# Gate and up projections as seven half-size products of 2x2 blocks, with two of the four weight sums made by accumulating transfers

## The chip, the core and the metric

The kernel runs on one core of one Trainium2 chip. A core has TensorE (matmuls, results in PSUM), VectorE (DVE in the profile), ScalarE (ACT), GpSimd (POOL) and SyncE (SP, which here only issues transfers), one instruction stream each, synchronised by semaphores, and 16 DMA engines. The metric is the device time of one launch in microseconds, as the median of several runs.

## The reference

One encoder layer on 512 tokens of 1024 channels, all in float32: a mixing part (a gated linear recurrence branch and a delta-rule branch), then a SwiGLU feed-forward part, with RMS norms. What the change touches is the feed-forward part:

```
x = x + (g_rnn * y_rnn + g_dn * y_dn) @ w_out[l]
h = rmsnorm(x, ffn_norm[l])
gu = h @ w_gate_up[l]                    # 1024 x 5632
gt, up = jnp.split(gu, 2, axis=-1)       # 2816 columns each
x = x + (jax.nn.silu(gt) * up) @ w_down[l]
return rmsnorm(x, final_norm)
```

## The kernel before

All large products are made from float32 operands split in a high part (rounded to the matmul's fp32r format) and a low part (what is left), as three matmuls: high by high, high by low, low by high. Activations lie with channels on partitions and the 512 tokens along the free dimension.

`Plan` (L56) records every instruction of all engines first, with an estimated cost, a wanted time (`plan.t`) and the tiles that it touches. `order` (L147) then makes a list schedule: each engine takes the most urgent instruction whose operands and tile buffers are there, and the instructions are emitted in that order, fixed for each engine. `spend` (L431) moves the wanted time on by the time that TensorE is to take, and starts a new stage; the first 172 stages, all up to the output projection, have their priorities in the list `TIMES`, the later ones go by the running time. Weights are loaded some 40 us ahead of their wanted time and split `AHEAD` = 12 us ahead. A transfer is planned with its issue cost, 1.4 us, its bytes at 360 GB/s times 1.25, and 0.9 us; VectorE's and ScalarE's costs are taken 10% high, POOL's 20%. `Rec.call` (to L372) holds the costs and makes every instruction, so nearly all rows of the profile have the line L372, and groups are told apart by tiles.

The tiles: `wraw` (3 buffers, a weight block as loaded), `whi` and `wlo` (2 each, its parts), `graw` (1), `t2` (14 of 128x512) and `t4` (22 of 128x1024); both of the last appear as `t` in the profile. PSUM has 3 banks `mm`, 3 `ax` and 2 `st`.

The feed-forward part: `norm_transpose` (L488) scales and transposes two chunks of 128 tokens at a time on TensorE (by a diagonal matrix `dg`), and makes `hh2` and `hl2`, high and low parts (ScalarE the high, VectorE the low). Then, for each of `NF` = 22 blocks of 128 outputs, gate and up (L1195 on): load a 1024x128 block (512 KB) on SP's queue, cast it on ScalarE, subtract on VectorE, and accumulate 24 matmuls of 512 columns in `mm3` (L589), or twice 24 of 256 columns for the first two blocks (`parts` 2), so that the first can begin before all tokens are normed. After both, ScalarE makes the silu, VectorE the product, and `split` its two parts, in `fa[n]`. The down projection (L1211 on) goes over pairs of these blocks, in two halves of 512 output columns, with each chunk of tokens as the stationary operand.

Of the kernel before, what the change touches and what calls it, by code (L numbers as in the profile page):

```python
# [10 lines left out]
ALU = mybir.AluOpType  # L11
# [44 lines left out]
class Plan:  # L56
    """Records the engines' instructions in program order, then emits them in the order of a list schedule: each engine
    takes the most urgent instruction whose operands and tile slots are there."""
# [8 lines left out]
    def __init__(self, nc):  # L67
        self.nc = nc
        self.ops = []
        self.where, self.bases = [], []  # L70
        self.t = self.base = 0.0
        self.stage = 0
        self.tags = {}
        self.tile_tag = {}
        self.hist = {}
        self.keep = set()
        self.extra = ()
        self.admit = ()

# [242 lines left out]
class Rec:  # L322
    """One engine of a Plan: a call is recorded, not made."""
# [4 lines left out]
    def __getattr__(self, op):  # L328
        real = getattr(self.real, op)

        def call(*a, **kw):
# [46 lines left out]
def trunk(ctx: ExitStack, tc: tile.TileContext, x, mix_norm, w_in, rg_conv_w, rg_conv_b, rg_wa, rg_ba, rg_wx, rg_bx,  # L378
# [64 lines left out]
    # ------------------------------------------------------------ constants  # L443
# [16 lines left out]
    # ------------------------------------------------------------ x, norm, transpose  # L460
# [27 lines left out]
    def norm_transpose(srcs, dgs, gain_, hh, hl, c0):  # L488
        """Two chunks of tokens, scaled, to channels on partitions, times the norm's weights, in high and low parts."""
        for k2 in range(KD // 2):  # L490
# [28 lines left out]
    # ------------------------------------------------------------ per-channel parameters  # L519
# [45 lines left out]
    # ------------------------------------------------------------ projections  # L565
# [3 lines left out]
    def stage(src, shape, view=lambda t: t, admit=()):  # L569
        """A block of weights in its high and low parts: the load and the split run ahead of the products."""  # L570
# [46 lines left out]
    # ------------------------------------------------------------ DeltaNet gates, token-major, columns (dir, head, chunk)  # L617
# [61 lines left out]
    # ------------------------------------------------------------ RG-LRU  # L679
# [67 lines left out]
    # ------------------------------------------------------------ gates and branch projections  # L747
# [9 lines left out]
    # ------------------------------------------------------------ DeltaNet  # L757
# [112 lines left out]
        # back to rows on partitions: tb[0] the inverses, tb[1] their transposes  # L870
# [16 lines left out]
        # level 64  # L887
# [28 lines left out]
        # level 128  # L916
# [123 lines left out]
    # ------------------------------------------------------------ order of the mixing part  # L1040
# [99 lines left out]
    # ------------------------------------------------------------ output projection, residual, norm  # L1140
# [41 lines left out]
    ws = [weights_w(wo_part(k2, 1)) for k2 in range(4)]  # L1182
    for c in range(NT):
# [5 lines left out]
        if c % 2:  # L1189
            norm_transpose(x1[c - 1:c + 1], dgs[c - 1:c + 1], gain2, hh2, hl2, c - 1)  # L1190
# [3 lines left out]
    fa = []  # L1194
    for n in range(NF):  # L1195
        pos = []
        for c0 in (n * P, D_FF + n * P):
            spend(5.2)
# [6 lines left out]
        V.tensor_tensor(s_, s_, pos[1], ALU.mult)  # L1205
# [4 lines left out]
    ssf = small([P, NT, 3], "ssf", 1)  # L1210
    def down_mm(po, c, k2, hi, lo, n0=0, n=512):  # L1211
        spend(1.3 * n / 512)
        cs_ = slice(c * P, (c + 1) * P)
        for k in (2 * k2, 2 * k2 + 1):
            T.matmul(po[:, 0:n], fa[k][:, 0, cs_], hi[:, k % 2, n0:n0 + n], start=k == 0, stop=False)
            T.matmul(po[:, 0:n], fa[k][:, 0, cs_], lo[:, k % 2, n0:n0 + n], start=False, stop=False)
            T.matmul(po[:, 0:n], fa[k][:, 1, cs_], hi[:, k % 2, n0:n0 + n], start=False, stop=k == NF - 1)
# [10 lines left out]
    # (chunk, first column, columns) of each accumulation: the last one's end is all that the output waits for  # L1228
# [65 lines left out]
```

## Time and profile before

| | |
|---|---|
| median of 3 runs | 1113.97 us (1112.96 to 1114.12) |
| span of the profiled execution | 1112.2 us |
| mean granted TensorE clock | 0.998 |
| second norm and blocks 0 and 1 of gate and up | 740.6 to 767.5 us |
| blocks 2 to 21 | 767.5 to 985.1 us |
| down projection, last norm, stores | 985.1 to 1112.2 us |

The rows of the profile give start, duration, engine, operation, the written tile, the read tiles, shape and count. Groups give the busy time and the mean in ns, then the idle time of that engine just before them and what ended it. A matmul's duration is its time through the array; matmuls overlap, so the time that one costs is the distance between starts. PEld is TensorE's weight load.

### The profile page before, as it was taken

How to read it: one execution, taken by the hardware profiler on the slowest of the kernel's cores; microseconds unless marked ns; L12 is line 12 of the kernel's file. 1: busy time of each engine (PE TensorE's matmuls, PEld its weight loads, DVE VectorE, ACT ScalarE, POOL GpSimd, SP SyncE). 2: the span in 40 equal slices, each digit the busy share in tenths (PEclk: the TensorE clock that was granted, in tenths of full speed). 3: DMA queues.
4: the chain of work that ended last, by engine and by line, in shares of the span. 5: the costliest groups of instructions: out<-in, count | busy, mean ns of one | idle time of the engine just before them, and what ended most of it. 6: DMA issues, size and time to landing. Idle time of an engine off the chain costs nothing.

```text
span 1112.2 us, 15808 instructions
## 1 busy us (share of the span) xinstructions
PE 1087.8 (98%) x6228; PEld 915.5 (82%) x6228; DVE 703.1 (63%) x1230; ACT 577.1 (52%) x1000; POOL 44.5 (4%) x93
## 2 busy tenths in 40 slices
PE   7999999999999999999999999999999999999997
PEld 6988788878888887888788796889888888888886
DVE  5777999699985988698579748653333333332432
ACT  6868988876358546584754434343323232321223
POOL 2000000002010100210010000000000000000000
PEclk9999999999999999999999999999999999999999
DMA  7342323223321142023212213513333333323322
GB/s 196 91 112 76 95 77 93 73 78 107 85 77 53 29 138 77 22 74 95 59 34 78 82 36 129 175 38 95 95 95 95 95 98 102 104 89 101 114 95 76
DMA packets 160778, 98.29 MB, mean 88 GB/s; under 512 B 4800, under 2 KB 151344, under 8 KB 160704
## 3 DMA queue, kind: packets, MB, share of 16 engines
q1 hardware_dynamic: 159232, 93.99, 29.6%
q10 hardware_dynamic: 1184, 3.15, 0.8%
q8 instruction: 49, 0.80, 0.3%
q0 software_dynamic: 288, 0.13, 0.1%
q14 instruction: 25, 0.20, 0.1%
HBM read 95.17 MB, written 2.10 MB: 87 GB/s over the span
## 4 chain that ended last, share of the span: by engine, by line
PE 83%; DVE 3%; ACT 2%; issue 0%; DVEq 0%; ACTq 0%
PE mm L372 59%; PE st L372 12%; PE ax L372 12%; DVE t L372 3%; ACT na L372 1%; ACT t L372 1%; DVE wlo L372 0%; ACT ax L372 0%; ACT whi L372 0%; ACT L372 0%; DVE na L372 0%; DVEq L1289 0%; ACT drt L372 0%; ACT rst L372 0%; DVE nq L372 0%
## 5 line engine op out<-in xcount | busy, mean ns | idle before, releaser
L372 DVE TENSOR_TENSOR wlo<-wraw,whi 128x1024 fp32r<-128x1024 f32 (+2 forms) x171 | 196.1, 1148 | 264.8 <-PE mm L372 147.8
L372 PE MATMUL mm<-hh,whi 128*128 128x512 f32 (+2 forms) x896 | 334.1, 378 | 1.1 <-ACT whi L372 1.1
L372 PE MATMUL mm<-hl,whi 128*128 128x512 f32 (+2 forms) x896 | 333.8, 377 | 0.0
L372 ACT CAST whi<-wraw 128x1024 fp32r<-128x1024 f32 (+2 forms) x172 | 169.8, 988 | 286.3 <-PE mm L372 202.3
L372 PE MATMUL mm<-hh,wlo 128*128 128x512 f32 (+1 forms) x880 | 211.5, 378 | 1.1 <-DVE wlo L372 1.1
L372 PEld LDWEIGHTS mm<-hh,whi 128*128 128x128 f32 (+1 forms) x896 | 167.9, 187 | 31.2 <-ACT whi L372 1.9
L372 PEld LDWEIGHTS mm<-hl,whi 128*128 128x128 f32 (+1 forms) x896 | 167.9, 187 | 29.5 <-DVE hl L372 0.2
L372 DVE TENSOR_TENSOR t<-t,t 128x512 fp32r<-128x512 f32 (+18 forms) x365 | 173.5, 485 | 26.8 <-ACT t L372 22.4
L372 PEld LDWEIGHTS mm<-hh,wlo 128*128 128x128 f32 x880 | 158.0, 188 | 31.1 <-DVE wlo L372 1.5
L372 PE MATMUL mm<-t,whi 128*128 128x512 f32 x320 | 81.8, 397 | 2.6 <-ACT t L372 1.8
L372 DVE SCALAR_TENSOR_TENSOR t<-mm,par,t 128x511 f32<-128x511 f32 (+1 forms) x108 | 79.7, 741 | 3.6 <-ACT t L372 2.9
L372 ACT ACT_TABLE_LOAD x58 | 74.4, 1283 | 5.8 <-PEq L1280 1.7
L372 PEld LDWEIGHTS mm<-t,whi 128*128 128x128 f32 x320 | 59.9, 190 | 17.0 <-ACT t L372 2.4
L372 ACT CAST t<-t 128x512 fp32r<-128x512 f32 x62 | 38.3, 617 | 64.5 <-DVE t L372 64.2
L372 PE MATMUL ax<-t,t 32*32 32x32 f32 (+3 forms) x642 | 57.9, 254 | 0.6 <-issue 0.5
L372 PEld LDWEIGHTS ax<-t,t 32*32 32x32 f32 (+1 forms) x642 | 44.7, 139 | 8.0 <-ACT t L372 1.6
L372 PE MATMUL st<-whi,t 128*128 128x512 f32 (+1 forms) x152 | 46.8, 367 | 0.0
L372 PE MATMUL ax<-whi,t 128*128 128x512 f32 (+1 forms) x152 | 46.6, 366 | 0.0
L372 ACT ACTIVATE t<-t 128x128 f32<-128x128 f32 (+3 forms) x64 | 37.4, 602 | 15.2 <-DVE t L372 12.1
L372 PE MATMUL mm<-t,wlo 128*128 128x512 f32 x160 | 43.1, 396 | 0.0
L372 PE MATMUL st<-hh,whi 128*128 128x512 f32 (+1 forms) x112 | 42.1, 380 | 0.0
L372 PE MATMUL st<-hl,whi 128*128 128x512 f32 (+1 forms) x112 | 41.8, 377 | 0.0
(172 smaller groups left out, 1299.0 us busy)
## 6 DMA issues: line engine op xcount, KB each, us to landing
wraw<-in_w_in_dram SPq DMA_DIRECT2D x72, 512.0 KB, 3.9
wraw<-in_w_gate_up_dram SPq DMA_DIRECT2D x44, 512.0 KB, 3.9
wraw<-in_w_down_dram SPq DMA_DIRECT2D x22, 512.0 KB, 3.7
wraw<-in_w_rnn_proj_dram SPq DMA_DIRECT2D x16, 384.0 KB, 3.4
wraw<-in_w_out_dram SPq DMA_DIRECT2D x8, 512.0 KB, 4.6
wraw<-in_w_dn_proj_dram SPq DMA_DIRECT2D x8, 384.0 KB, 3.4
t<-in_x_dram SPq DMA_DIRECT2D x4, 512.0 KB, 5.1
na<-in_x_dram ACTq DMA_DIRECT2D x4, 512.0 KB, 7.2
```

Source lines behind the costliest of these rows:

```text
L372: self.plan.add(e, lambda: real(*a, **kw), outs, ins, cost, tail, table)
```

## The change

For blocks 2 to 21, gate and up together are seen as one 2x2 block product. The weight is [[G1, G2], [U1, U2]], where G is the gate's and U the up projection's block of 128 outputs, and 1 and 2 are the halves of the 1024 inputs; the activation has the two halves of the inputs by the two halves of the tokens, 256 each. Seven products of a 512x128 weight by a 512x256 activation take the place of eight. They need four sums of weights, here named t1 = G1 + U1, t3 = U1 + U2, t2 = t1 + U2 and t4 = t2 + G2, four differences of activations, made once, and additions of the results.

- t1 and t3 come from transfers: SP loads G1 and U1 into the two halves of one `wraw` tile, and POOL's queue adds U1 and U2 onto them in the tile (`accum_op`). t2 and t4 are VectorE adds. G is loaded whole and split as before; U2 is loaded by itself in `graw`. Seven weights are split in parts, on ScalarE and VectorE.
- `norm_transpose` also writes an unsplit copy of the second norm's result (`whole`) in four `t4` tiles, from which the differences `q5`, `q7`, `q6`, `q3` are made and split while blocks 0 and 1 run. Those two blocks both go in halves of 256 columns, as before.
- The output of a block is left unsplit in `fa`, with the two token halves swapped for odd blocks, and is split a pair at a time in the down projection (`split_pair`); part of the low halves takes the place of `hh2` and `hl2`.
- The planner's fixed cost of one fp32r matmul is 13.3 ns, for 2.5, from the second half of the output projection on.

Comments are taken out too, which does nothing. The core of the diff:

```diff
-                    cost = max(n / 2.4, 107 if rhs.dtype == F32R else 54) + 2.5
+                    cost = max(n / 2.4, 107 if rhs.dtype == F32R else 54) + (self.plan.fixed if rhs.dtype == F32R else 2.5)
...
                 V.scalar_tensor_tensor(hl[:, kt, c0 * P:(c0 + 2) * P], pv, gain_[:, kt:kt + 1], f(ho), ALU.mult, ALU.subtract)
+                if whole:
+                    A.activation(whole[kt // 4][:, kt % 4, :], pv, AF.Copy, scale=gain_[:, kt:kt + 1])
...
     ws = [weights_w(wo_part(k2, 1)) for k2 in range(4)]
+    plan.fixed = 13.3
+    a1 = [four(shape=(P, 4, 256)) for _ in range(2)]
+    a2 = [four(shape=(P, 4, 256)) for _ in range(2)]
...
+    def parts_of(src, hi, lo, ahead):
+        now = plan.t
+        plan.t = now - ahead
+        A.copy(hi, src)
+        V.tensor_tensor(lo, src, f(hi), ALU.subtract)
+        plan.t = now
...
-            mm3(po, hi, lo, lambda k: hh2[:, k, :], lambda k: hl2[:, k, :], KD, 2 if n < 2 else 1)
+            mm3(po, hi, lo, lambda k: hh2[:, k, :], lambda k: hl2[:, k, :], KD, 2)
...
-        y = four(F32R)
-        split(s_, y)
-        fa.append(y)
...
+    (a11, a12), (a21, a22) = a1, a2
+    q5, q6, q7, q3 = (four(shape=(P, 4, 256)) for _ in range(4))
+    qs = {}
+    for name, q, x_, y_ in (("5", q5, a21, a22), ("7", q7, a11, a21), ("6", q6, a11, q5), ("3", q3, a12, q6)):
+        V.tensor_tensor(q, x_, y_, ALU.subtract)
+        qh, ql = four(F32R, (P, 4, 256)), four(F32R, (P, 4, 256))
+        A.copy(qh, q)
+        V.tensor_tensor(ql, q, f(qh), ALU.subtract)
+        qs[name] = (qh, ql)
...
+    def product(po, w, x_, start):
+        (wh, wl), (xh, xl) = w, x_
+        for k in range(4):
+            T.matmul(po, wh[:, k, :], xh[:, k, :], start=start and k == 0, stop=False, skip_group_check=not start)
+            T.matmul(po, wh[:, k, :], xl[:, k, :], start=False, stop=False, skip_group_check=not start)
+        for k in range(4):
+            T.matmul(po, wl[:, k, :], xh[:, k, :], start=False, stop=k == 3, skip_group_check=not start)
+
+    def gate_up(n):
+        spend(10.2)
+        now = plan.t
+        rg = new(wp, (P, 8, P), "wraw", 3)
+        b22 = new(wp, (P, 4, P), "graw", 1)
+        t2_, t4_ = two(shape=(P, 4, P)), two(shape=(P, 4, P))
+        t13 = new(wp, (P, 8, P), "wraw", 3)
+        wu = wg[:, :, D_FF + n * P:D_FF + (n + 1) * P]
+        plan.t = now - 44
+        Q.dma_start(t13[:, 0:4, :], wg[:, 0:4, n * P:(n + 1) * P])
+        Q.dma_start(t13[:, 4:8, :], wu[:, 0:4, :])
+        G.dma_start(t13, wu, accum_op=ALU.add)
+        plan.t = now - 40
+        Q.dma_start(rg, wg[:, :, n * P:(n + 1) * P])
+        Q.dma_start(b22, wu[:, 4:8, :])
+        t1, t3 = t13[:, 0:4, :], t13[:, 4:8, :]
+        plan.t = now - 24
+        V.tensor_tensor(t2_, t1, b22, ALU.add)
+        V.tensor_tensor(t4_, t2_, rg[:, 4:8, :], ALU.add)
+        plan.t = now
+        gh_, gl_ = new(wp, (P, 8, P), "whi", 2, F32R), new(wp, (P, 8, P), "wlo", 2, F32R)
+        parts_of(rg, gh_, gl_, AHEAD)
+        w7 = {"1": (gh_[:, 0:4, :], gl_[:, 0:4, :]), "2": (gh_[:, 4:8, :], gl_[:, 4:8, :])}
+        ah, al = new(wp, (P, 8, P), "whi", 2, F32R), new(wp, (P, 8, P), "wlo", 2, F32R)
+        bh, bl = four(F32R, (P, 8, P)), four(F32R, (P, 8, P))
+        for i, (name, src, hi, lo) in enumerate((("6", t2_, ah, al), ("7", t3, ah, al), ("5", t1, bh, bl), ("4", t4_, bh, bl))):
+            j = 4 * (i % 2)
+            w7[name] = hi[:, j:j + 4, :], lo[:, j:j + 4, :]
+            parts_of(src, *w7[name], AHEAD - 1.4 * i)
+        w7["3"] = two(F32R, (P, 4, P)), two(F32R, (P, 4, P))
+        parts_of(b22, *w7["3"], AHEAD - 7)
...
+        product(pa, w7["1"], xs7["1"], True)
+        A.copy(e[:, 0, :], pa)
+        product(pb, w7["6"], xs7["6"], True)
+        m = e[:, 1, :]
+        V.tensor_tensor(m, pb, e[:, 0, :], ALU.subtract)
+        product(pc, w7["7"], xs7["7"], True)
+        V.tensor_tensor(u[:, hi_], m, pc, ALU.subtract)
+        product(pa, w7["2"], xs7["2"], False)
+        act(s_[:, lo_], pa, AF.Silu)
+        product(pd_, w7["5"], xs7["5"], True)
+        V.tensor_tensor(u[:, hi_], pd_, u[:, hi_], ALU.add)
+        product(pc, w7["4"], xs7["4"], False)
+        V.tensor_tensor(s_[:, hi_], pc, m, ALU.subtract)
+        act(s_[:, hi_], s_[:, hi_], AF.Silu)
+        product(pd_, w7["3"], xs7["3"], False)
+        V.tensor_tensor(u[:, lo_], pd_, m, ALU.add)
+        V.tensor_tensor(fa[n // 2][:, n % 2, :], s_, u, ALU.mult)
...
+            fh = four(F32R)
+            fl = four(F32R) if j < 3 else keep[(j - 3) // 4][:, 2 * ((j - 3) % 4):, :][:, 0:2, :]
+            A.copy(fh, fa[j])
+            V.tensor_tensor(fl, fa[j], f(fh), ALU.subtract)
```

More of the change, by code (lines that the diff above doesn't have):

```diff
@@ L78, in __init__ @@
         self.admit = ()
+        self.fixed = 2.5
     def tile(self, pool, shape, dt, tag, bufs, name):
@@ L1204, in trunk @@
         act(s_, pos[0], AF.Silu)
-        V.tensor_tensor(s_, s_, pos[1], ALU.mult)
-        y = four(F32R)
-        split(s_, y)
-        fa.append(y)
+        for h in range(2):
+            o = 256 * (h ^ n % 2)
+            V.tensor_tensor(fa[n // 2][:, n % 2, o:o + 256], s_[:, h * 256:(h + 1) * 256], pos[1][:, h * 256:(h + 1) * 256], ALU.mult)
+    for n in range(BRIDGE):
+        if n % 2 == 0:
+            fa[n // 2] = four()
+        gate_up_plain(n)
+    (a11, a12), (a21, a22) = a1, a2
@@ new lines, in gate_up @@
+    def gate_up(n):
[29 more added lines that the diff above has]
+        parts_of(b22, *w7["3"], AHEAD - 7)
+        A_, B_, C_, D_ = (mmb(), stb(), axb(), axb() if n % 2 else mmb())
+        e, s_, u = two(shape=(P, 2, 256)), two(), two()
+        if n % 2 == 0:
+            fa[n // 2] = four()
+        pa, pb, pc, pd_ = (t[:, 0:256] for t in (A_, B_, C_, D_))
+        lo_, hi_ = (slice(0, 256), slice(256, 512)) if n % 2 == 0 else (slice(256, 512), slice(0, 256))
+        product(pa, w7["1"], xs7["1"], True)
[15 more added lines that the diff above has]
+        V.tensor_tensor(fa[n // 2][:, n % 2, :], s_, u, ALU.mult)
@@ L1209, in trunk, with split_pair @@
+    for n in range(BRIDGE, NF):
+        gate_up(n)
     wdn = w_down[0].rearrange("(k p) n -> p k n", p=P)
     ssf = small([P, NT, 3], "ssf", 1)
+    pairs = {}
+    keep = [new(hp, (P, KD, S), "hh", 1, F32R), new(hp, (P, KD, S), "hl", 1, F32R)]
+    def split_pair(j):
+        if j not in pairs:
+            now = plan.t
+            plan.t = now - AHEAD
+            fh = four(F32R)
+            fl = four(F32R) if j < 3 else keep[(j - 3) // 4][:, 2 * ((j - 3) % 4):, :][:, 0:2, :]
+            A.copy(fh, fa[j])
+            V.tensor_tensor(fl, fa[j], f(fh), ALU.subtract)
+            pairs[j] = fh, fl
+            plan.t = now
+        return pairs[j]
@@ L1211, in down_mm @@
     def down_mm(po, c, k2, hi, lo, n0=0, n=512):
         spend(1.3 * n / 512)
[L1213 removed]
+        fh, fl = split_pair(k2)
         for k in (2 * k2, 2 * k2 + 1):
[L1215 to L1217 removed]
+            c_ = (c + 2 * (k % 2)) % NT
+            xh, xl = (t[:, k % 2, c_ * P:(c_ + 1) * P] for t in (fh, fl))
+            T.matmul(po[:, 0:n], xh, hi[:, k % 2, n0:n0 + n], start=k == 0, stop=False)
+            T.matmul(po[:, 0:n], xh, lo[:, k % 2, n0:n0 + n], start=False, stop=False)
+            T.matmul(po[:, 0:n], xl, hi[:, k % 2, n0:n0 + n], start=False, stop=k == NF - 1)
```

14 lines of the change are left out of this document (9 added, 5 removed).

## The prediction

> **What bounds the kernel now.** I read the page's head and its chain first, then the windows by stage, then the timeline of TensorE inside the stage that is changed.
>
> ```profile
> span 1112.2 us, 15808 instructions
> ...
> PE 1087.8 (98%) x6228; PEld 915.5 (82%) x6228; DVE 703.1 (63%) x1230; ACT 577.1 (52%) x1000; POOL 44.5 (4%) x93
> ...
> PE 83%; DVE 3%; ACT 2%; issue 0%; DVEq 0%; ACTq 0%
> ```
> ```profile
> 752.28 232.99 PE mm L372 x1088
> ```
> ```profile
> core 0: us, PE busy (x) PEld busy (x) DVE busy (x) ACT busy (x) POOL busy (x), PEclk, DMA share, GB/s
> ...
> 740.00:767.50 27.50, 27.50 (x233) 27.39 (x232) 11.43 (x21) 12.69 (x22) 0.00 (x0) 1.00 0.21 58
> 767.50:985.00 217.50, 217.50 (x962) 180.10 (x961) 74.70 (x80) 66.81 (x81) 0.00 (x0) 1.00 0.33 97
> 985.00:1104.00 119.00, 119.00 (x581) 100.77 (x580) 36.55 (x46) 30.20 (x42) 0.00 (x0) 1.00 0.29 93
> ```
>
> The longest piece of the chain that ended last is one unbroken run of 1088 matmuls, the gate and up projections. In the windows TensorE is busy for the whole of that stage at full clock, while VectorE is busy 34%, ScalarE 31% and the DMA engines 33%. So this stage is worth what its matmuls take, and nothing else in it costs anything yet. How long one takes is read from starts, since the durations overlap:
>
> ```profile
> 753.08 0.28 PE L372 MATMUL mm<-hh,whi 128*128 128x256 f32 x1
> ...
> 755.96 0.28 PE L372 MATMUL mm<-hh,whi 128*128 128x256 f32 x1
> ```
> ```profile
> 772.95 0.39 PE L372 MATMUL mm<-hh,whi 128*128 128x512 f32 x1
> ...
> 778.39 0.39 PE L372 MATMUL mm<-hh,whi 128*128 128x512 f32 x1
> ```
>
> Between the two rows of each pair stand 24 matmuls, one accumulation. With 256 columns (the first two blocks of 128 outputs, which already go in halves) it takes 2.88 us, 120.0 ns each; with 512 columns 5.44 us, 226.7 ns each. Half the columns cost 53%, not 50%: some 13 ns stay on each matmul. The weight load is busy 27.39 of 27.50 us where the columns are 256, so nothing is left there to hide it better.
>
> **The products.** Blocks 2 to 21 (20 of them) now take 48 matmuls of 512 columns: 48 x 226.7 = 10.88 us (217.5 / 20 agrees). Seven products of four blocks of k in three parts are 84 matmuls of 256: 84 x 120.0 = 10.08 us. That is 0.80 us a block, 16.0 us over 20. An eighth of the arithmetic goes, but only 7.4% of the time, since the 13 ns are paid 84 times for 48. Blocks 0 and 1 keep their halves.
>
> The Trainium skill ("TensorE: Matmul & The Clock Gate", Back-to-back issue gap) gives N / 2.4 + 2.5 ns, that is 215.8 and 109.2 ns: by it a block would win 1.19 us and the stage 23.7 us. Both measured spacings are 11 ns longer, which counts against the form with more matmuls, so I keep 16.0.
>
> **VectorE and ScalarE in the new stage.** The groups of the stage, and three instructions back to back:
>
> ```profile
> L372 DVE TENSOR_TENSOR wlo<-wraw,whi 128x1024 fp32r<-128x1024 f32 x40 | 49.0, 1224 | 125.6 <-PE mm L372 122.6 <-ACT whi L372 3.0
> L372 ACT CAST whi<-wraw 128x1024 fp32r<-128x1024 f32 x41 | 43.2, 1053 | 89.1 <-PE mm L372 89.1
> L372 DVE TENSOR_TENSOR t<-t,t 128x512 fp32r<-128x512 f32 x20 | 13.8, 692 | 13.1 <-ACT t L372 13.1
> ...
> L372 ACT CAST t<-t 128x512 fp32r<-128x512 f32 x20 | 12.4, 621 | 51.0 <-DVE t L372 51.0
> ```
> ```profile
> 756.23 0.69 DVE L372 TENSOR_TENSOR t<-t,mm 128x512 f32<-128x512 f32 x1 [2.54 <-PE mm L372]
> 756.83 1.22 DVE L372 TENSOR_TENSOR wlo<-wraw,whi 128x1024 fp32r<-128x1024 f32 x1
> 757.97 0.68 DVE L372 TENSOR_TENSOR t<-t,t 128x512 fp32r<-128x512 f32 x1
> ```
> ```profile
> L372 DVE TENSOR_TENSOR na<-ax,na 128x256 f32<-128x256 f32 x1 | 0.4, 425 | 0.2 <-PE ax L372 0.2
> ```
>
> Start to start VectorE needs 0.60 us for 512 columns and 1.14 for 1024; for 256 I take 0.425 less the same overlap of 0.085, 0.34 us. A block has two weight sums (1.20), the low part of eight blocks of k (1.14), five low parts of four (3.00), five half-width adds on the results (1.70) and the last multiply (0.60): 7.64 us of 10.08, 76% (8.9 us if durations, not spacings, counted). ScalarE: 1.05 + 5 x 0.62 + three half-width passes of about 0.40 = 5.35 us, 53%. Neither is the bound by sum. What matters is order: both work strictly in the order that the planner wrote. The tightest place is the fifth product's add (`u` from `pd_`): the seventh product accumulates into the same bank, and only the sixth, 1.44 us, stands between. The planner's lags are 0.25 and 0.32 us and the add 0.43, so 0.44 us are left, and VectorE is often inside a piece of 0.6 or 1.14 us. Behind a late add wait the third product and the output multiply. Between 0 (another product is put first) and 0.8 us (a whole wide piece less the cover) a block, I take 0.15: 3 us in all.
>
> **Into and out of the stage.** The second norm's transposition gains 16 copies of 128x256 on ScalarE, behind which the square sum of the last chunk of tokens can queue:
>
> ```profile
> 737.81 2.30 ACT L372 ACTIVATE hh<-ax,gain 128x256 fp32r<-128x256 f32 x6 [2.50 <-PE ax L372]
> ...
> 741.76 1.06 ACT L372 ACTIVATE t<-na 128x1024 f32<-128x1024 f32 x1
> ```
> ```profile
> 743.47 0.29 DVE L372 TENSOR_SCALAR dg<-ident,rin 128x128 f32<-128x128 f32 x1
> ```
> ```profile
> 744.99 2.84 PE L372 MATMUL ax<-dg,na 128*128 128x128 f32 x24
> ```
>
> A copy takes 2.30 / 6 = 0.38 us. Sixteen for the first two chunks' high parts and copies end at about 737.8 + 6.1 = 743.9, so the square starts 2.1 us later, the scale at 745.6 instead of 743.47. TensorE reaches those transpositions at 744.99 and has 12 of its 48 first-half matmuls left then, 1.44 us: cost 0 to 2 us, I take 1. Then four token differences with their parts: eight VectorE passes of 1.14 (9.1 us) and four ScalarE casts, in the 27.5 us of blocks 0 and 1, where VectorE is busy 11.4; with block 2's weights (about 5 us) it comes to 26 of 27.5. Cost 0 to 3 us (products that need no difference can go first), I take 1. The output parts, formerly split in the stage, are split in the down projection: 11 pairs, 11 x 1.05 on ScalarE and 11 x 1.22 on VectorE, beside 119 us of matmuls that leave them 89 and 82 us idle: nothing, or 2.3 us if the first pair comes late.
>
> **The transfers.** A block loads 1.25 MB plainly (before: 1 MB) and adds 512 KB through POOL's queue.
>
> ```profile
> q1 hardware_dynamic: 38528, 20.97, 32.6%
> ...
> wraw<-in_w_gate_up_dram SPq DMA_DIRECT2D x36, 512.0 KB, 3.9
> ```
> ```profile
> q0 software_dynamic: 288, 0.13, 1.2%
> ...
> t<-in_dn_conv_w_dram POOLq DMA_DIRECT2D x1, 48.0 KB, 6.3
> ```
> ```profile
> 5.08 0.53 POOL L372 DMA_DIRECT2D t<-in_dn_conv_w_dram  x1
> ```
>
> The stage's 40 loads took 32.6% of 217.5 us, 1.77 us of all 16 engines each; 2.5 of them are 4.43 us a block. The before trace has no accumulating transfer. Its engine time lies between a plain 512 KB, 1.77 us, and twice what POOL's small packets cost (1.2% of the first 60 us for 0.13 MB, 2.9 us per 512 KB; twice, because the destination is read too), 5.8 us. The DMA engines are then 62% to 101% busy. I take 3.5, nearer the plain row since the packets are of that size: 79%. From issue to landing it takes between 0.53 + 3.9 = 4.4 us and 6.3 + 5.8 = 12.1; I take 6.5. The planner expects 5.3 (1.2 issue, 1.4, 1.8, 0.9), so I see it 1.2 us late, within VectorE's spare 2.4 us a block and ahead of the weights' use: 0, up to the third rival's price.
>
> **Sum** against the profiled execution: 1112.2 - 16.0 + 3 + 1 + 1 = 1101.2 us. The median of the runs, 1113.97, is 1.8 us above that execution's span; so 1103.0 us.
>
> **Rivals.** *VectorE late for its own adds.* Every block loses 0.5 us at the fifth or seventh product, as VectorE at 76% in fixed order has no room for a piece of 1.14 us in front of the add. For: the 0.44 us of cover. Against: list scheduling puts ready products first, and the planner prices VectorE 10% high. 1112.2 - 16 + 10 + 2 + 1.8 = 1110.0 us.
>
> *The accumulating transfer is late* (the slow side). The sum `t2_` is VectorE's first reader of it and is placed by the planner where the transfer ought to land. If it takes 8.9 us, 3.6 more than planned, VectorE stands at `t2_`, and behind it stand the adds and low parts of the block that TensorE is in. From the release of a load buffer to that sum pass two blocks, so each carries half, 1.8 us, less the 0.44 of cover: 1.36 us a block, 27 in all: 1112.2 - 16 + 27 + 2 + 1.8 = 1127.0. At 5.3 + 2 x (0.44 + 0.70) = 7.6 us from issue to landing it eats the whole gain; beyond that the change loses. For: 6.3 us even for 48 KB. Against: that was behind the loads of x at the start, and `b22`'s one buffer holds `t2_` back in any case. The Trainium skill ("Collectives: The Full Stack", The bandwidth ceiling) says that an add in a transfer halves the rate because of its second read; no run here shows it yet. By it the engine time is 3.54 us, inside my bounds.
>
> *The planner's new order costs elsewhere* (four more tiles out of 22 held from the output projection on, gate-up loads asked for 44 us ahead): the part before 740 us loses some 8 us, 1111.2. For: greedy lists jump. Against: the first 172 stages keep their priorities.
>
> **Chances.** Forecast 0.52, VectorE late 0.16, transfer late 0.22, order elsewhere 0.10. A measurement of this kernel tells 0.2%, 2.2 us, from no change. Faster: 0.52, two thirds of 0.16 and half of 0.10, 0.66 rounded down for spread; same 0.08, from the second and the fourth; slower 0.27, the transfer and the rest of the order. The low end is the products alone, 1112.2 - 16 + 1.8 = 1098; the high end takes in three quarters of the transfer's case, 1126. Forecast's own: 1098 to 1108.
>
> **What would show it.** Right: TensorE unbroken in the new stage, 1.44 us a product, the stage 202 to 206 us long, VectorE near 76%, transfers landing within 7 us. Wrong: gaps before the seventh product, with VectorE as releaser; VectorE idle on a DMA at the weight sums; DMA share above 0.9; a later start of the stage than 740.6.

## The result, and the profile after

| | before | after |
|---|---|---|
| median of 4 runs each | 1113.72 us (1112.96 to 1114.12) | 1124.7 us (1123.78 to 1127.17) |
| ratio | 1 | 1.0102, 95% interval 1.0088 to 1.0117 |
| span of the profiled execution | 1112.2 us | 1125.4 us |
| first product of block 2 | 767.5 us | 774.66 us |
| first matmul of 512 columns in the down projection | 985.1 us | 996.46 us |

The change makes the kernel 1.0% slower, 11 us; the forecast was 1103.0. The profiled execution is the slowest of the four, 1127.17 us, 2.5 above the median. Its page:

```profile
span 1125.4 us, 17863 instructions
...
PE 1080.2 (96%) x6948; PEld 939.0 (83%) x6948; DVE 808.6 (72%) x1449; ACT 625.6 (56%) x1129; POOL 79.8 (7%) x113
...
PE 62%; DMA 12%; DVE 8%; ACT 4%; issue 3%; DVEq 0%; SPq 0%; POOLq 0%; ACTq 0%
```

TensorE's busy time fell by 7.6 us, and yet the span grew by 13.2. In the chain of work that ended last TensorE's share went from 83% to 62%, and transfers, which its line did not list before, now have 12%. The windows of the changed stage (columns as before: busy us and count of each engine, then granted clock, DMA share, GB/s):

```profile
740.00:767.50 27.50, 24.29 (x179) 21.79 (x179) 18.17 (x31) 19.93 (x41) 0.00 (x0) 1.00 0.18 41
767.50:800.00 32.50, 26.88 (x219) 26.10 (x217) 20.70 (x33) 13.79 (x23) 4.63 (x3) 1.00 0.72 143
800.00:850.00 50.00, 47.94 (x394) 47.31 (x394) 39.21 (x69) 22.75 (x42) 6.17 (x4) 1.00 0.84 174
850.00:900.00 50.00, 45.76 (x372) 44.61 (x371) 35.77 (x63) 22.20 (x41) 7.69 (x5) 1.00 0.83 158
900.00:950.00 50.00, 47.60 (x389) 46.59 (x388) 36.59 (x65) 21.33 (x40) 6.18 (x4) 1.00 0.85 175
```

At 120.0 ns a matmul 50 us hold 417; here stand 372 to 394. No other engine is full, and the clock is at its full rate. What TensorE lacks is operands. The waits from 775 to 985 us (engine, line, waited for; total us, times, longest) say whose:

```profile
POOL wraw L373 <- DVE t L373: 103.6, 11, 10.4
POOL wraw L373 <- DMA wraw<-in_w_gate_up_dram: 56.7, 6, 10.8
ACT t L373 <- DMA wraw<-in_w_gate_up_dram: 52.6, 15, 6.3
DVE t L373 <- DMA wraw<-in_w_gate_up_dram: 38.8, 19, 6.9
...
PE ax L373 <- DVE t L373: 9.6, 11, 3.5
```
```profile
L373 DVE TENSOR_TENSOR t<-wraw,graw 128x512 f32<-128x512 f32 x20 | 13.8, 692 | 38.6 <-DMA wraw<-in_w_gate_up_dram 38.5
```

The last row is one form of one operation, the sum `t2_`: VectorE stands 38.5 us in front of it, 1.9 us a block, waiting for a transfer into `wraw`, and TensorE then waits for VectorE (9.6 us in the last row of the waits). Which transfer it is can be read from one turn of the load buffers (start, us, engine, operation and tiles):

```profile
831.18 2.28 SPq L373 DMA_DIRECT2D wraw<-in_w_gate_up_dram  x3
...
839.02 1.56 POOL L373 DMA_DIRECT2D wraw<-in_w_gate_up_dram  x1 [9.39 <-DVE t L373]
...
845.37 0.69 DVE L373 TENSOR_TENSOR t<-wraw,graw 128x512 f32<-128x512 f32 x1 [1.88 <-DMA wraw<-in_w_gate_up_dram]
...
852.72 1.23 DVE L373 TENSOR_TENSOR wlo<-wraw,whi 128x1024 fp32r<-128x1024 f32 x1 [0.26 <-ACT whi L373]
...
853.98 2.28 SPq L373 DMA_DIRECT2D wraw<-in_w_gate_up_dram  x3
```

SP loads as soon as a buffer is free. The last of the three loads is issued by 833.46 us and lands some 5 us later (landings below); then POOL issues the accumulate (its row names a VectorE instruction as releaser, but the loads come last), and 6.35 us later VectorE's sum begins; from 812 us on it does so 6.2 to 6.6 us after the issue in every block, which is the time that an accumulate takes to land. So the transfer that VectorE waits for at `t2_` is the accumulate itself. The low part that frees the next buffer stands behind that sum in VectorE's order. Such a turn takes 22.8 us here and serves two blocks, and two blocks of products take 20.16. The transfers from 780 to 960 us, by queue (packets, MB, share of the 16 engines) and by kind of issue (KB, median us from issue to landing):

```profile
q1 hardware_dynamic: 43157, 21.56, 45.0%
q0 software_dynamic: 16640, 8.39, 38.0%
...
wraw<-in_w_gate_up_dram SPq DMA_DIRECT2D x34, 256.0 KB, 5.0
wraw<-in_w_gate_up_dram SPq DMA_DIRECT2D x16, 512.0 KB, 5.1
wraw<-in_w_gate_up_dram POOLq DMA_DIRECT2D x16, 512.0 KB, 6.3
graw<-in_w_gate_up_dram SPq DMA_DIRECT2D x17, 256.0 KB, 3.8
```

q0 is POOL's queue, the accumulating transfers: 0.380 x 180 us for 8.39 MB is 4.28 us of all 16 engines per 512 KB. SP's plain loads beside them take 0.450 x 180 for 21.56 MB, 1.97 us per 512 KB. A plain 512 KB load lands after 5.1 us; in the kernel before it was 3.9.

The 13.2 us, by places in the two traces:

- The stage starts 774.66 - 767.5 = 7.2 us later.
- 20 blocks without a stall are 20 x 10.08 = 201.6 us, for 217.6 before: -16.0.
- The stage is in fact 996.46 - 774.66 = 221.8 us long, and one product (1.44 us) falls behind that mark: 221.8 + 1.44 - 201.6 = 21.6 us of stalls, 1.08 a block.
- Behind it are left 1125.4 - 996.46 - 1.44 = 127.5 us, against 127.1: 0.4.

So 7.2 - 16.0 + 21.6 + 0.4 = 13.2.

### The profile page after: what moved, and what is told of

Its sections match the earlier page's. It is cut to its first block, busy times and chain, and to the rows that moved or that the text cites. A ratio compares the mean times of both kernels' runs of the same rounds, so it can differ in the third digit from the quotient of the medians.

```text
span 1125.4 us, 17863 instructions
## 1 busy us (share of the span) xinstructions
PE 1080.2 (96%) x6948; PEld 939.0 (83%) x6948; DVE 808.6 (72%) x1449; ACT 625.6 (56%) x1129; POOL 79.8 (7%) x113
## 4 chain that ended last, share of the span: by engine, by line
PE 62%; DMA 12%; DVE 8%; ACT 4%; issue 3%; DVEq 0%; SPq 0%; POOLq 0%; ACTq 0%
PE mm L373 37%; PE ax L373 13%; PE st L373 12%; DMA wraw<-in_w_gate_up_dram 10%; DVE t L373 6%; ACT t L373 2%; DMA graw<-in_w_gate_up_dram 2%; DVE wlo L373 2%; ACT whi L373 1%; DMA wraw<-in_w_out_dram 1%; ACT na L373 0%; ACT ax L373 0%; DVE hl L373 0%; ACT hh L373 0%; ACT L373 0%
## 5 line engine op out<-in xcount | busy, mean ns | idle before, releaser
L373 DVE TENSOR_TENSOR wlo<-wraw,whi 128x1024 fp32r<-128x1024 f32 (+3 forms) x171 | 185.0, 1084 | 126.2 <-ACT whi L373 83.6
L373 ACT CAST whi<-wraw 128x1024 fp32r<-128x1024 f32 (+3 forms) x172 | 160.8, 936 | 188.8 <-PE mm L373 105.1
L373 PE MATMUL mm<-hh,whi 128*128 128x512 f32 (+2 forms) x736 | 250.6, 352 | 1.1 <-ACT whi L373 1.1
L373 PE MATMUL mm<-hl,whi 128*128 128x512 f32 (+2 forms) x736 | 250.0, 352 | 0.4 <-DVE hl L373 0.4
L373 PE MATMUL mm<-hh,wlo 128*128 128x512 f32 (+1 forms) x720 | 158.7, 352 | 1.1 <-DVE wlo L373 1.1
L373 PEld LDWEIGHTS ax<-t,t 128*128 128x128 f32 (+1 forms) x876 | 74.5, 153 | 14.9 <-DVE t L373 6.9
L373 PE MATMUL mm<-t,t 128*128 128x256 f32 (+1 forms) x372 | 67.2, 324 | 5.6 <-DVE t L373 5.4
L373 ACT CAST t<-t 128x512 fp32r<-128x512 f32 (+1 forms) x75 | 51.9, 703 | 36.3 <-DVE t L373 35.3
L373 PEld LDWEIGHTS mm<-t,t 128*128 128x128 f32 x372 | 54.5, 190 | 12.6 <-DVE t L373 7.5
L373 ACT ACTIVATE t<-t 128x128 f32<-128x128 f32 (+4 forms) x84 | 45.8, 558 | 27.6 <-DVE t L373 24.4
```

Source lines behind the costliest of these rows:

```text
L373: self.plan.add(e, lambda: real(*a, **kw), outs, ins, cost, tail, table)
```

## The experiments

The theory after the first look: the 21.6 us are the price of the accumulating transfers. It leaves open through what: the time of the DMA engines, which the other loads then lack; the longer way of one buffer (load, accumulate, sum, parts) in a loop over three buffers; the planner's too low price for them, and so the order; or not they at all, but VectorE, which has more to do. The 7.2 us before the stage are a question of its own. "Stage" is below the time from the first product of block 2 to the first down matmul of 512 columns (one or two products of 1.44 us fall behind it: one in the change and without accumulates, two with all sums on VectorE). The medians are of 4 runs, with the plain transfer of 5 and with half of 6; the ratio is to the kernel before with its 95% interval. Stages and DMA shares (850 to 900 us) are of the profiled execution; the change's is 2.5 us above its median, so some 2 us of a difference to its stage may be spread between executions:

| run | median us | ratio | block 2 starts | stage us | DMA share |
|---|---|---|---|---|---|
| after | 1124.7 | 1.0102 (1.0088 to 1.0117) | 774.66 | 221.8 | 0.83 |
| no accumulates | 1104.85 | 0.9923 (0.9908 to 0.9938) | 774.14 | 200.6 | 0.44 |
| accumulates at twice the price | 1122.05 | 1.0078 (1.0061 to 1.0096) | 774.09 | 216.5 | 0.88 |
| all sums on VectorE | 1103.72 | 0.9907 (0.9890 to 0.9923) | 773.50 | 198.7 | 0.36 |
| norm copy on GpSimd | 1122.73 | 1.0082 (1.0067 to 1.0097) | 769.49 | 222.2 | 0.90 |
| plain on POOL's queue | 1110.13 | 0.9969 (0.9956 to 0.9982) | 773.95 | 205.5 | 0.63 |
| four buffers | 1141.12 | 1.0250 (1.0235 to 1.0265) | 797.63 | 211.9 | 0.82 |
| half accumulated | 1110.23 | 0.9969 (0.9957 to 0.9980) | 774.67 | 204.6 | 0.68 |
| sums on VectorE, copy on GpSimd | 1099.24 | 0.9871 (0.9854 to 0.9887) | 768.75 | 198.7 | 0.36 |
| accumulates aside | 1160.39 | 1.0414 (1.0396 to 1.0432) | none comparable | | 0.48 |
| aside, one a block | 1121.69 | 1.0064 (1.0043 to 1.0085) | 773.15 | 218.2 | 0.89 |
| aside, two tiles | 1132.22 | 1.0166 (1.0149 to 1.0183) | 774.70 | 227.1 | 0.86 |

### No accumulates

```diff
-        G.dma_start(t13, wu, accum_op=ALU.add)
```

t1 and t3 are then G1 and U1 alone; all else stays.

> The accumulating transfers are left out, so t1 is G1 and t3 is U1 and the products are of other weights; all else, the 84 matmuls of a block too, stays. Theory A (VectorE stands in its fixed order at the sum t2, 1.9 us a block in the changed kernel, because the transfer lands later than planned): the 20 blocks take some 205 us for 223, the whole about 1107 us. Rival B (VectorE, at 76%, is late for its own adds on the results): the stage stays above 218 us, the whole above 1119. Rival C (the DMA engines or the three load buffers bound the stage): as A, since the traffic falls too.

Measured: 1104.85 us (1104.47 to 1105.95), the stage 200.6. Its window:

```profile
775.00:850.00 75.00, 75.00 (x628) 75.00 (x627) 63.38 (x113) 37.56 (x69) 0.00 (x0) 1.00 0.47 134
```

TensorE is busy for 75.00 of 75.00 us, 628 matmuls at 119 to 120 ns, with VectorE at 63.38 / 75 = 85%. The products cost what was forecast, and VectorE is late for nothing: all but 0.5 us (200.62 + 1.44 - 201.6) of the 21.6 hang on that one transfer a block. SP's loads into `wraw`, from 780 to 960 us, land sooner too:

```profile
wraw<-in_w_gate_up_dram SPq DMA_DIRECT2D x18, 512.0 KB, 3.8
wraw<-in_w_gate_up_dram SPq DMA_DIRECT2D x34, 256.0 KB, 4.5
```

VectorE's order of work in a block is another one here, so this run alone doesn't part the transfer from the order.

### Accumulates at twice the price

```diff
-                tail = max(out.nbytes() / 360.0, 1)
+                tail = max(out.nbytes() / 360.0, 1) * (2 if "accum_op" in kw else 1)
```

> The same work and transfers; only the planner's price of an accumulating transfer's bytes is doubled, so that it expects one to land 1.8 us later than before and writes another order. Theory A: the order goes around the wait, VectorE's idle time on the transfer falls from 38 us to under 15, the 20 blocks take 205 to 210 us for 223, the whole 1107 to 1112. Rival B: no change, 1122 to 1127. Rival C (DMA engines or load buffers bound): the wait moves but the stage keeps over 218 us, the whole over 1119.

Measured: 1122.05 us (1120.32 to 1124.86), the stage 216.5, 5.3 less; VectorE's wait for transfers into `wraw` falls from 38.8 to 24.0 us, but the accumulates now land after 8.8 us and SP's 512 KB loads after 6.6. A higher price gives the planner an order that stands somewhat less. The median is 2.6 us lower, with ranges that overlap, far from the 1107 to 1112 expected if the order were the cause. The work to be moved is still there; the order is a small part.

### All sums on VectorE

```diff
-        b22 = new(wp, (P, 4, P), "graw", 1)
-        t2_, t4_ = two(shape=(P, 4, P)), two(shape=(P, 4, P))
-        t13 = new(wp, (P, 8, P), "wraw", 3)
+        t2_, t4_, t3 = (two(shape=(P, 4, P)) for _ in range(3))
+        ru = new(wp, (P, 8, P), "wraw", 3)
...
-        G.dma_start(t13, wu, accum_op=ALU.add)
...
-        Q.dma_start(b22, wu[:, 4:8, :])
-        t1, t3 = t13[:, 0:4, :], t13[:, 4:8, :]
+        Q.dma_start(ru, wu)
+        t1, b22 = ru[:, 0:4, :], ru[:, 4:8, :]
...
+        V.tensor_tensor(t3, t1, b22, ALU.add)
+        V.tensor_tensor(t1, t1, rg[:, 0:4, :], ALU.add)
```

Gate and up are each loaded once, whole, 1 MB a block as before the change.

> All four sums of weights on VectorE, no accumulating transfer, 1 MB of loads a block as before the change; VectorE then has 7.64 + 1.20 = 8.84 us of work in a block of 10.08, 88%. Theory A: no transfer to stand at, the 20 blocks take 204 to 212 us, the whole 1106 to 1113. Rival B (VectorE's load): the stage gets longer than the 223 us of the changed kernel, the whole above 1126. Rival C: as A.

Measured: 1103.72 us (1102.08 to 1104.01). The windows:

```profile
775.00:850.00 75.00, 75.00 (x627) 75.00 (x627) 69.33 (x125) 38.81 (x70) 0.00 (x0) 1.00 0.38 112
850.00:900.00 50.00, 50.00 (x419) 50.00 (x419) 45.45 (x81) 23.94 (x46) 0.00 (x0) 1.00 0.36 106
```

VectorE is busy 92% and 91% of the time in a fixed order, and TensorE has no gap. The two sums that the transfers were to take off VectorE cost nothing on it. The theory that VectorE's load makes the stalls falls.

### Plain on POOL's queue, and half accumulated

```diff
-        G.dma_start(t13, wu, accum_op=ALU.add)
+        G.dma_start(t13, wu)
```

The transfer overwrites t1 and t3 with U1 and U2 instead of adding: the same queue, bytes, buffers and waits, without the second read.

> The transfer on POOL's queue writes U1 and U2 over the tile instead of adding them, so the sums t1 and t3 are not formed and the products are of other weights; place, bytes, descriptors and waits stay. Theory A1 (the read-modify-write is what is slow: 4.3 us of all engines for 512 KB against 1.9 for a plain load, 6.3 us from issue to landing): the engine time falls to about 2, landing to 5 us or less, the 20 blocks take 203 to 208 us for 222, the whole 1106 to 1111. Theory A2 (any third transfer in the chain, load, then POOL, then sum, with its issue and landing, is too long for three load buffers): the stage stays at 215 us or more, the whole over 1117.

```diff
-        G.dma_start(t13, wu, accum_op=ALU.add)
+        G.dma_start(t13[:, 0:4, :], wu[:, 0:4, :], accum_op=ALU.add)
...
+        V.tensor_tensor(t3, t3, b22, ALU.add)
```

Only t1 comes from an accumulating transfer, of 256 KB; t3 is a sum on VectorE.

> Only t1 = G1 + U1 is made by an accumulating transfer (256 KB a block); t3 = U1 + U2 goes to VectorE (0.60 us more, 8.24 of 10.08 a block). If the price follows the bytes that are added (A1): half of the 21 us between the changed kernel and the one with all sums on VectorE, the whole about 1113 us. If it is a fixed latency in the order (A2): 1119 or more, as each block keeps one such wait. Below 1107 would say that neither holds and that only the full size is too much.

Measured: 1110.13 and 1110.23 us, the stages 205.5 and 204.6. The transfers from 780 to 960 us, first of the plain one, then of the half:

```profile
q1 hardware_dynamic: 45375, 22.67, 44.6%
q0 software_dynamic: 2592, 9.44, 17.4%
...
wraw<-in_w_gate_up_dram SPq DMA_DIRECT2D x18, 512.0 KB, 3.9
wraw<-in_w_gate_up_dram POOLq DMA_DIRECT2D x18, 512.0 KB, 4.6
```
```profile
q1 hardware_dynamic: 45670, 22.82, 44.5%
q0 software_dynamic: 9504, 4.72, 21.6%
...
wraw<-in_w_gate_up_dram SPq DMA_DIRECT2D x18, 512.0 KB, 3.7
```

Plain, a 512 KB transfer on POOL's queue takes 0.174 x 180 / 18 = 1.74 us of the engines, in 144 packets; with the addition 4.28 us in 1040 packets of 504 bytes, 2.5 times as much. SP's 512 KB loads land after 3.9 us again. VectorE's order of work in a block is the change's in the plain run, so the order is out as the cause of the difference between these two. Of the 19.9 us between the change and the run without accumulates, 14.6 (1124.7 - 1110.1) belong to the addition, with its smaller packets and its later landing (6.3 us for 4.6), and 5.3 to a further transfer and step in the loop. Half the accumulated bytes cost 1110.2 - 1103.7 = 6.5 us of 21.0, less than half; 1113 had been expected if the price followed the bytes. The share of the engines alone doesn't set the price: at 0.63 (plain) and 0.68 (half) the stages are 205.5 and 204.6 us.

### Four buffers

`wraw` gets four buffers for three everywhere, paid for with two of `t2` (12 for 14).

> Four load buffers for three everywhere (room is made by 12 small tiles for 14), accumulating transfers as in the changed kernel. Theory A2 (the chain of load, accumulating transfer, sums and parts holds its buffer too long): the accumulating transfer starts earlier, VectorE's idle time on it falls from 38 to under 15 us, the 20 blocks take 203 to 210 us for 222. Theory A1 (engine time of the transfers, 84% busy): the buffers only move the wait, the stage stays over 215 us, the whole over 1117.

Measured: 1141.12 us. The planner's order in front of the stage became worse (block 2 starts at 797.6 us), so the median doesn't answer the question. The stage by itself does in part: 211.9 us, 9.9 less than in the change, at the same DMA share (0.82). The loop over three buffers seems to have a share in the stalls, as far as a run with another order can say, and with a fourth some 10 us of them stay.

### Accumulates aside

What parts the engines' time from the wait for the buffer: t1 and t3 are again G1 and U1 alone, and the accumulating transfer goes onto a tile that no one reads.

```diff
+    side = four(shape=(P, 8, P))
+    G.memset(side, 0.0)
...
-        G.dma_start(t13, wu, accum_op=ALU.add)
+        G.dma_start(side, wu, accum_op=ALU.add)
```

> The accumulating transfers stay, 512 KB a block onto the same queue, but into a tile of their own that nothing in the stage reads, so no weight sum, no part and no load buffer waits for one; t1 and t3 are then G1 and U1 alone, as where the accumulates were left out. Theory A (their engine time slows every load, and this alone makes the stalls): the DMA share stays near 0.84 and the landing of SP's loads near 5.0 us in the window 780 to 960, the stage stays at 215 us or more, the time above 1117. Theory B (the wait for the added-on buffer, through issue and 6.3 us of landing in a loop over three load buffers, makes the stalls): the DMA share stays near 0.84 too, but the stage is 201 to 206 us and the time 1104 to 1108. Between 206 and 215 us both have a part, in the proportion of the stage's excess over 200.6.

Measured: 1160.39 us; the run missed its question. With nothing to wait for, all 20 accumulates ran between 540 and 711 us, ahead of the stage, and the part in front of the stage became longer, by a way that was not followed up. Two of its rows are of use, the landing on the page and a window:

```profile
t<-in_w_gate_up_dram POOLq DMA_DIRECT2D x20, 512.0 KB, 6.3
```
```profile
850.00:900.00 50.00, 50.00 (x419) 50.00 (x419) 41.58 (x74) 24.49 (x46) 0.00 (x0) 1.00 0.48 138
```

From 540 to 711 us the DMA share was 0.65, and POOL's queue took 49.5% of 171 us for the 20 accumulates, 4.2 us each. An accumulate lands after 6.3 us in that quieter stretch as well, just as in the change; so neither figure comes from the crowd in the changed stage. And with the accumulates gone from it the stage has no gaps.

### Accumulates aside, one a block

```diff
-        G.dma_start(t13, wu, accum_op=ALU.add)
...
         V.tensor_tensor(t2_, t1, b22, ALU.add)
+        G.tensor_copy(a21[:, 0, 0:1], t2_[:, 0, 0:1])
+        G.dma_start(a21.rearrange("p a (b c) -> p (a b) c", c=P), wu, accum_op=ALU.add)
```

`a21` is one of the unsplit norm copies, dead once the differences are made; the copy of one column ties each accumulate to its block. In a second form `a21` and `a22` take turns.

> t1 and t3 are G1 and U1 alone, as where the accumulates were left out. One accumulating transfer of 512 KB a block stays in the stage, onto a tile that nothing reads any more; a copy of one column on GpSimd makes it wait for its block's t2, so that there is one a block. No weight sum, part or load buffer waits for it. Theory A (the engine time of the accumulates, which slows every load, makes the stalls): DMA share 0.8 or more in 780 to 960, SP's loads landing in 4.8 to 5.2 us, the stage 212 us or more, the time above 1115. Theory B (the loop through the added-on load buffer makes them, and the loads alone would have time enough): DMA share 0.8 as well, but the stage 200 to 204 us and the time 1104 to 1108. Between 204 and 212 both have a part, in proportion to the stage's excess over 200.6.

> As the run before (t1 and t3 are G1 and U1 alone; one accumulating transfer a block that nothing in the stage reads), but onto two such tiles by turns, so that GpSimd's small copy, which holds t2, waits for the accumulate before the last and not for the last: their chain of 10.56 us a block, longer than a block's 10.08, is gone. Theory A (traffic alone): the DMA share stays at 0.85 or more and the stage stays at 212 us or more, against 218.2. Theory B (what cost time in that run was the chain of the copies, and in the change it is the wait for the added-on buffer): the stage is 200 to 206 us. Between, both, in proportion.

Measured: 1121.69 us with a stage of 218.2, and 1132.22 us with one of 227.1. The last part of both stages doesn't count: the tiles `a21` and `a22` are taken again there, and instructions stand until the accumulates into them have landed (VectorE 6.9 us at 972 us in the first form; ScalarE 5.2 us at 968 and VectorE 7.0 at 983 in the second). So here are the windows from 800 to 950 us, in which only GpSimd's own small copies wait for an accumulate: the change, no accumulates, one tile, two tiles.

```profile
800.00:950.00 150.00, 141.31 (x1149) 138.50 (x1149) 111.57 (x196) 66.28 (x123) 20.04 (x13) 1.00 0.84 169
```
```profile
800.00:950.00 150.00, 149.80 (x1248) 149.59 (x1248) 119.74 (x208) 71.65 (x133) 0.00 (x0) 1.00 0.47 132
```
```profile
800.00:950.00 150.00, 146.15 (x1202) 144.50 (x1202) 112.07 (x197) 69.72 (x128) 28.77 (x28) 1.00 0.90 177
```
```profile
800.00:950.00 150.00, 141.01 (x1143) 137.77 (x1142) 107.29 (x187) 64.49 (x120) 27.43 (x28) 1.00 0.83 166
```

With two tiles TensorE stands 9.0 us of 150, in the change 8.7, without accumulates 0.2. The transfers of the two-tile run from 780 to 960 us, and two of its waits from 775 to 1000:

```profile
q1 hardware_dynamic: 43040, 21.50, 44.9%
q0 software_dynamic: 17231, 8.68, 39.1%
...
t<-in_w_gate_up_dram POOLq DMA_DIRECT2D x17, 512.0 KB, 8.0
wraw<-in_w_gate_up_dram SPq DMA_DIRECT2D x16, 512.0 KB, 6.6
wraw<-in_w_gate_up_dram SPq DMA_DIRECT2D x32, 256.0 KB, 6.6
```
```profile
POOL t L373 <- DVE t L373: 156.1, 18, 11.6
...
DVE t L373 <- DMA wraw<-in_w_gate_up_dram: 36.7, 25, 3.6
```

`wraw` holds nothing but plain loads here, and POOL waits for VectorE, not the other way. Yet VectorE stands 36.7 us for `wraw`, about as long as in the change (38.8), since SP's loads now land after 6.6 us, for 3.8 and 4.5 without accumulates. So the traffic alone can make stalls of this size. The share alone doesn't set them: with one tile it is higher, 0.90, and TensorE stands only 3.9 us. There each accumulate waits for the one before on the same tile, is issued 10.6 us after it on the mean and lands after 9.6. What makes the difference between the two forms was not tried by itself. In the change slower loads and the wait for the accumulate stand in one and the same loop, and no run parts their shares.

### Norm copy on GpSimd, alone and with the sums on VectorE

```diff
-                if whole:
-                    A.activation(whole[kt // 4][:, kt % 4, :], pv, AF.Copy, scale=gain_[:, kt:kt + 1])
...
+        if whole:
+            for i in range(2):
+                for j in range(2):
+                    a, b = (t[:, 4 * i + 2 * j:4 * i + 2 * j + 2, c0 * P:(c0 + 2) * P] for t in (hh, hl))
+                    G.tensor_tensor(whole[i][:, 2 * j:2 * j + 2, :], f(a), f(b), ALU.add)
```

The unsplit copy is then the sum of the two parts, made on GpSimd in four pieces, and ScalarE's second pass over the PSUM bank is gone.

> The unsplit copy of the second norm's result is made by POOL as high plus low part, out of SBUF, instead of by 16 more ScalarE passes over the PSUM banks that VectorE reads too. Theory D (the 6 us lost between the second norm and block 2 come from ScalarE and VectorE taking turns on one bank, which the copy in the middle lengthens): block 2 begins at 768 to 770 us instead of 774.7, the whole about 1119 us. Rival E (they come from the load of VectorE and ScalarE by the four differences and their parts): block 2 stays within 1.5 us of 774.7, the whole 1123 to 1126.

> All four sums on VectorE and the unsplit copy of the norm on POOL. If the two causes are separate and add up, block 2 begins at 769 us instead of 773.5 and the 20 blocks stay at 200 us: 1103.7 - 4.5 = about 1099 us. If the time won before block 2 is lost again, because VectorE (88% busy in the stage) starts it with more work behind: 1102 to 1105.

Measured alone: block 2 starts at 769.49 us, 5.2 earlier, with the stalls of the stage as in the change; 1122.73 us, 2.0 below the change where some 5 were expected (the spans of the profiled executions differ by 5.1). With the sums on VectorE: 1099.24 us (1098.96 to 1099.64), 0.9871 of before, 25.5 us below the change, and the fastest of all. Three timelines from behind the norm's first transposition: ScalarE in the change, VectorE in the change, and ScalarE with the copy on GpSimd (start, us, engine, operation and tiles, idle before and its releaser):

```profile
739.03 0.48 ACT L373 ACTIVATE hh<-ax,gain 128x256 fp32r<-128x256 f32 x1 [2.50 <-PE ax L373]
739.40 0.47 ACT L373 ACTIVATE t<-ax,gain 128x256 f32<-128x256 f32 x1
740.42 0.47 ACT L373 ACTIVATE hh<-ax,gain 128x256 fp32r<-128x256 f32 x1 [0.55 <-DVE hl L373]
740.80 0.47 ACT L373 ACTIVATE t<-ax,gain 128x256 f32<-128x256 f32 x1
```
```profile
739.91 0.48 DVE L373 SCALAR_TENSOR_TENSOR hl<-ax,gain,hh 128x256 fp32r<-128x256 f32 x1 [2.69 <-ACT t L373]
741.30 0.48 DVE L373 SCALAR_TENSOR_TENSOR hl<-ax,gain,hh 128x256 fp32r<-128x256 f32 x1 [0.91 <-ACT t L373]
```
```profile
738.54 2.30 ACT L373 ACTIVATE hh<-ax,gain 128x256 fp32r<-128x256 f32 x6 [2.50 <-PE ax L373]
```

With the copies ScalarE makes one high part and one copy, then waits 0.55 us for VectorE's low part, and VectorE waits 0.91 us for ScalarE's copy. Without them six high parts go in one run of 2.30 us, as before the change. The run takes away the copies' own time and these waits together and doesn't part the two.

## Why the prediction was wrong, step by step

**The products** (-16.0): right. With the sums on VectorE the stage has 10.08 us a block: 198.7 us and two products of 1.44 behind it are 201.6. 50 us hold 419 matmuls, 119 ns apart. The Trainium skill ("TensorE: Matmul & The Clock Gate", Back-to-back issue gap) gives N / 2.4 + 2.5 ns, 109.2 ns here, for a single matmul by itself and not for a stream with weight loads; at that spacing they would be 458. The prediction held it against a stream, and was right to leave it out of its sum.

**VectorE late for its own adds** (+3): nothing was lost, even at 92% busy. The sum of 7.64 us a block was low, since in the run without accumulates VectorE has 63.38 + 39.13 = 102.5 us busy in 125, 8.3 a block, but room was left. This rival (1110.0) is out.

**The transfers** (0): the step that failed. "So I see it 1.2 us late, within VectorE's spare 2.4 us a block and ahead of the weights' use: 0." It measured 21.6 us. The landing was taken well (6.5, measured 6.3), and the engine time within its bounds (3.5 taken, 4.28 measured). What went wrong is what they were used for. The prediction set the accumulate's 1.2 us against VectorE's spare time, and let the plain loads land as before. But VectorE can't use spare time while it stands, in its fixed order, at `t2_`, and the low part behind that sum frees the buffer for the next loads. So what counts is the whole turn of the buffers, load, accumulate, sum and low part: it takes 221.8 / 10 = 22.2 us for two blocks, and the products need 20.16. Both of its transfers were later than planned: the accumulate landed after 6.3 us for 5.3, and the 256 KB loads ahead of it after 5.0 us, where the planner's prices give 3.7 (0.45 to issue, 1.4, 0.9 for the bytes and 0.9) and the run without accumulates 4.5. That is 2.3 us a turn or 1.2 a block, an estimate from these figures, against 1.08 measured. The engines' share was taken too low as well: at the planned pace a block's transfers take 2.5 x 1.97 + 4.28 = 9.2 us of the engines in 10.08, 91%, not the 79% forecast. Of the prediction's signs of being wrong, VectorE idle on a DMA at the weight sums did show. A share above 0.9 didn't, because the stalls stretched a block to 221.8 / 20 = 11.1 us: 9.2 of these are 83%, what the windows have. A share of a stage that already stalls understates what the stage at full pace would ask for.

The Trainium skill ("Collectives: The Full Stack", The bandwidth ceiling) explains the half rate of a ReduceScatter by the second read that its add needs. Here an add takes 4.28 us per 512 KB beside SP's plain loads of 1.97 in packets of much the same size, 2.2 times, and 2.5 times the plain transfer on its own queue: this kernel's transfer comes near that factor of two. The prediction had it as "inside my bounds" and drew nothing from it for the other loads.

**The rival of the late transfer** (1127.0) gave nearly the right size, 1.36 us a block for 1.08, and named the right place, `t2_`, and the turn of two blocks. Its condition was wrong: it took 8.9 us of landing for that price, and 7.6 as the point where the gain is gone, and all of the gain was gone at 6.3. It counted only the accumulate's lateness and not that of the loads in the same turn, so that its size came out near is in part luck.

**Into the stage** (1 + 1): the right place, too small. Block 2 starts 7.2 us late; 1.2 of these were there before the norm's first transposition (734.05 against 732.83 us) and 6.0 arose in the norm and the two blocks behind it. Taking the copy away from ScalarE brought back 5.2, of which 0.5 lay ahead of the norm (733.56), so 4.7 of the 6.0. The prediction counted ScalarE's 16 copies by their length; what it didn't count is that the two engines wait for each other over the bank, 0.55 and 0.91 us in the rows shown. How much of the 4.7 us is these waits and how much the copies' own time is not shown. For the differences at most the 1.3 us left remain.

**Down projection** (0): right, 127.5 us for 127.1. The planner's order elsewhere (1111.2): the 1.2 us before the norm are the most that it can have in the change, though the run with four buffers shows that the mechanism exists, 23 us at that place.

Put together with the right terms, 1112.2 - 16.0 + 7.2 + 21.6 + 0.4 = 1125.4, the change's span; the run without accumulates has 1103.4, near the forecast's 1101.2, since +3 for VectorE too much and 5.2 for the start of the stage too little nearly cancel, which is luck. (The prediction's chances of faster, same and slower, 0.66, 0.08 and 0.27, add to 1.01.)

What stays open: how the stalls of the change divide between slower loads and the wait for the accumulate, how much of the stalls four or more buffers would take away with an unharmed order in front of the stage, and what delays the 1.2 us before the norm.

## What to carry to other kernels

Before moving an add from a compute engine into a transfer, add up the engine time of all transfers of a stage at the pace that the stage is to have, the accumulate at more than twice a plain one. Here 91% at the planned pace went with slower loads. Then follow a load buffer once around, load, accumulate, the sum that reads it, and the work behind that sum which frees it, and set this against the pace: an engine that waits in a fixed order can't spend its spare time there. And look first whether that engine needs relief: here VectorE at 92% cost nothing, and with all four sums on it the same change is 0.9% faster than before instead of 1.0% slower (1.3% with the norm's copy on GpSimd too).

## What the hardware showed unexpectedly

- An accumulating transfer of 512 KB goes in 1040 packets of 504 bytes and takes 4.28 us of all 16 engines, the plain one on the same queue in 144 packets of 3.6 KB 1.74 us. Its issue on POOL takes longer too (group rows of the change and of the plain run):

```profile
L373 POOL DMA_DIRECT2D wraw<-in_w_gate_up_dram x20 | 30.9, 1546 | 367.8 <-DVE na L373 160.9 <-DVE t L373 136.9 <-DMA wraw<-in_w_gate_up_dram 56.7
```
```profile
L373 POOL DMA_DIRECT2D wraw<-in_w_gate_up_dram x20 | 17.8, 888 | 363.0 <-DVE t L373 163.6 <-DVE na L373 159.7 <-DMA wraw<-in_w_gate_up_dram 28.5
```

- ScalarE and VectorE, both reading one PSUM bank, waited for each other, 0.55 and 0.91 us in the rows above. The runs don't tell whether the bank or the semaphores between the instructions ask for it.
